# Packing the first row block of a float32 decoder trunk and fixing the order of its opening work

## The chip, the cores and the metric

The kernel runs on one core of one Trainium2 chip. The metric is the device time of one launch in microseconds, lower is better. It is measured from outside the program, so it is a little longer than the span in the profile, which runs from the first to the last instruction.

## The reference, cut to what matters

The program is one inference step of a one-layer convolutional decoder on 320 tokens (256 of a prompt, 8 groups of 8 new ones), all in float32:

```python
h = _rmsnorm(x, norm_mix_g)                      # x: 320 x 2048
proj = jnp.einsum('btd,dn->btn', h, w_in)        # w_in: 2048 x 14336
b_a, c_a, v_a, glu_a, glu_b, gate_a, gate_b = jnp.split(proj, IN_SPLITS, axis=-1)
conv_a, new_a = _causal_depthwise(c_a * v_a, buf_a, conv_a_w)
y_a = jnp.einsum('btc,cd->btd', b_a * conv_a, w_out_a)
u = glu_a * jax.nn.sigmoid(glu_b)
conv_b, new_b = _causal_depthwise(u, buf_b, conv_b_w)
...
x = x + jnp.einsum('btd,de->bte', merged, w_o)
h2 = _rmsnorm(x, norm_ffn_g)
ff = jax.nn.silu(jnp.einsum('btd,df->btf', h2, w_gate)) * jnp.einsum('btd,df->btf', h2, w_up)   # width 5632
x = x + jnp.einsum('btf,fd->btd', ff, w_down)    # then the final _rmsnorm
```

## The kernel before

**Products.** Every projection is computed in split precision: a weight w and an activation x are each cut into a "hi" part, rounded to TensorE's float32r, and a "lo" part, the float32 rest. Three products, hi·hi, hi·lo and lo·hi, stand for one (lines 221 to 223: `whi` with `rh`, `whi` with `rl`, `wlo` with `rh`). Each takes a stationary 128 x 128 weight tile and 320 moving columns, the tokens. Weights come from memory once, in *pieces* of 512 KB: four row slices k of 128 rows, 256 columns wide (tile `raw`, five buffers). ScalarE casts a piece to `whi` (line 181), VectorE subtracts to get `wlo` (line 185); there are three buffers of each. A *unit* is one output block of 256 columns; it has two accumulators in PSUM (one for each half j) and, for 2048 input rows, four pieces.

**The opening.** The weights cannot wait for the norm of x, so the first units multiply the x that is scaled by the norm's gain alone; the factor `rb`, one over the root mean square, is applied to the results. x is laid out as 16 chunks of 128 features by 320 tokens. For a chunk c, `x_chunk` makes `rh` on ScalarE (line 319) and `rl` on VectorE (line 320), and `x_square` squares it on ScalarE (line 326) and adds it up in `lnacc` on VectorE (lines 298 and 300). After the sixteenth square `x_factor` computes `rb`; `x_norm` then makes the normalized chunks that all later units use.

The first three units (two blocks of `glu_b`, one of `glu_a`) run as a group, so that a chunk of x feeds three units at once: `run_group` goes through row block 0 (chunks 0 to 3) slice by slice over the three units, and through row blocks 1 to 3 unit by unit. The callback `at_start(r, m, k)` is called ahead of row block r, unit m, slice k, and issues the x work and the splits of row block 0. From the fourth unit on, units run one after the other; each splits two pieces ahead and lets background tasks run (the 31-tap convolution of `glu_a * sigmoid(glu_b)` on VectorE, line 394, after ScalarE has copied its input into a window buffer `win`, line 386).

**What sets the order.** A list scheduler orders each engine's instructions by its own estimate of times; `tc.issue_after(x)` is a constraint on that order. At run time every engine works through its list in order and waits on semaphores. SyncE's queue issues nearly all transfers in program order, and each transfer uses one of eight semaphores in turn, so the ninth waits for the first. Ahead of the first product TensorE runs eleven products of an all-zero tile (`spin`, line 86), which VectorE clears first (line 83).

**The first transfers.** `lead` (the norm's gain and x chunk 0) on SyncE, the first slices of pieces 0 and 1 on ScalarE's queue, and then on SyncE, in turn, slices of pieces 0 to 2 and chunks of x, each its own transfer of 128 to 256 KB.

Of the kernel before, what the change touches and what calls it, by code (L numbers as in the profile page):

```python
# [8 lines left out]
F32 = mybir.dt.float32  # L9
# [3 lines left out]
ALU = mybir.AluOpType  # L13
# [19 lines left out]
SLOTS = 100  # L33
# [5 lines left out]
def trunk_kernel(ctx: ExitStack, tc: tile.TileContext, a):  # L39
# [33 lines left out]
    def xcol(c):  # L73
        return a["x"][:, NC + c * T : NC + (c + 1) * T]

    def load_x(cs):
        for c in cs:
            xc[c] = slot("xc")
            sp.dma_start(out=xc[c], in_=xcol(c))  # L79


    idle = slot("idle", F32R)
    ve.memset(idle.bitcast(F32), 0.0)
    o = pst("spin")
    for _ in range(11):
        first = te.matmul(o[:, :T], idle[:, 0:P], idle, start=True, stop=True, skip_group_check=True).ins
# [71 lines left out]
    def split_to(i):  # L158
        while nsplit[0] <= min(i, len(pieces) - 1):
# [7 lines left out]
            if nsplit[0] == 3:  # L167
                split(q, 0, 2)
                split(q, 2, 4)
            elif nsplit[0] > 3:  # L170
                split(q, 0, n)
# [6 lines left out]
    def hi_part(q, k0, k1, eng=None):  # L178
        ks = slice(k0, k1)
        f = ve.tensor_copy if eng is ve else ac.copy  # L180
        return f(out=q["hi"][:, ks, :], in_=q["raw"][:, ks, :]).ins  # L181
# [29 lines left out]
    def begin(u):  # L211
# [4 lines left out]
        def prod(q, k, j):  # L216
# [4 lines left out]
            te.matmul(o, wh, hi[kk], start=(kk == 0), stop=False)  # L221
            te.matmul(o, wh, lo[kk], start=False, stop=False)  # L222
            return te.matmul(o, wl, hi[kk], start=False, stop=(kk == nk - 1)).ins  # L223
# [5 lines left out]
    def run_group(us, at):  # L229

        on = [begin(u) for u in us]
        steps = [(0, m, k) for k in range(KP) for m in range(3)]
        steps += [(r, m, k) for r in range(1, NC // KP) for m in range(3) for k in range(KP)]
        for r, m, k in steps:
# [3 lines left out]
            if r:  # L238
                load_to(pi + DMA_AHEAD)
            at(r, m, k)  # L240
            if r and k == 0 or (r, m, k) == (0, 1, KP - 1):
                with tc.issue_after(x_last["ac"]), tc.issue_after(x_last["ve"]):
                    split_to(pi + 1 if r else 3)
# [52 lines left out]
    def csum(dst, src, c):  # L296
        if c == 0:
            ve.tensor_copy(out=dst, in_=src)
        else:
            ve.tensor_tensor(out=dst, in0=dst, in1=src, op=ALU.add)  # L300
# [748 lines left out]
```

## Time and profile before

| | us |
|---|---|
| median of 3 runs | 2079.13 |
| lowest and highest run | 2079.02, 2079.3 |
| the profiled execution | 2079.16 |
| its span | 2077.4 |
| TensorE busy | 2066.7 (99%) |
| VectorE busy | 1269.2 (61%) |
| ScalarE busy | 806.3 (39%) |

The profiled execution's time is 1.76 us more than its span; what is said of the span holds for the time when that difference stays. TensorE is called PE in the profile (PEld are its weight loads), VectorE DVE, ScalarE ACT, GpSimd POOL, SyncE SP; a q behind a name is that engine's queue of transfers. A row of the timeline gives the start and the duration in us, the engine, the line, the operation, out<-in, the shapes, how many instructions in a row were merged, and in brackets how long the engine was idle before and what ended that. Products overlap in the pipeline, so the pace is read from start to start, not from durations. A row of the tile view gives count, then least, median and longest duration in ns, then the first and the last start. A row of the window view gives the stretch, its length, the busy time of the five engines, TensorE's granted clock, the transfer engines' share, and GB/s.

### The profile page before, as it was taken

How to read it: one execution, taken by the hardware profiler on the slowest of the kernel's cores; microseconds unless marked ns; L12 is line 12 of the kernel's file. 1: busy time of each engine (PE TensorE's matmuls, PEld its weight loads, DVE VectorE, ACT ScalarE, POOL GpSimd, SP SyncE). 2: the span in 40 equal slices, each digit the busy share in tenths (PEclk: the TensorE clock that was granted, in tenths of full speed). 3: DMA queues.
4: the chain of work that ended last, by engine and by line, in shares of the span. 5: the costliest groups of instructions: out<-in, count | busy, mean ns of one | idle time of the engine just before them, and what ended most of it. 6: DMA issues, size and time to landing. Idle time of an engine off the chain costs nothing.

```text
span 2077.4 us, 33904 instructions
## 1 busy us (share of the span) xinstructions
PE 2066.7 (99%) x14097; PEld 2064.1 (99%) x14097; DVE 1269.2 (61%) x1854; ACT 806.3 (39%) x1170; POOL 4.4 (0%) x26
## 2 busy tenths in 40 slices
PE   9999999999999999999999999999999999999998
PEld 9999999999999999999999999999999999999998
DVE  7898889988986754345555645545334544544445
ACT  6544344444434344333344333333223333333432
POOL 0000000000000000000000000000000000000000
PEclk9999999999999999999999999999999999999999
DMA  8555544444444444444555444444454444444553
GB/s 268 155 173 155 183 143 153 153 152 145 155 152 150 145 151 153 149 147 151 158 172 169 151 152 148 148 151 147 143 157 152 152 149 147 151 152 143 153 149 107
DMA packets 98050, 321.17 MB, mean 155 GB/s; under 512 B 12936, under 2 KB 21192, under 8 KB 97864
## 3 DMA queue, kind: packets, MB, share of 16 engines
q1 hardware_dynamic: 97320, 318.35, 49.3%
q8 instruction: 110, 1.80, 0.4%
q10 hardware_dynamic: 576, 0.66, 0.1%
q14 instruction: 44, 0.36, 0.0%
HBM read 315.42 MB, written 4.98 MB: 154 GB/s over the span
## 4 chain that ended last, share of the span: by engine, by line
PE 99%; DMA 1%; DVE 0%; ACT 0%; SPq 0%; issue 0%; DVEq 0%
PE acc L223 33%; PE acc L221 33%; PE acc L222 32%; DMA raw<-in_w_in 1%; PE acc L695 0%; PE acc L697 0%; PE acc L696 0%; PE acc L700 0%; PE acc L701 0%; DVE yo L790 0%; DVE rl L320 0%; PE rbp L820 0%; DVE wlo L185 0%; SPq L146 0%; SPq L79 0%
## 5 line engine op out<-in xcount | busy, mean ns | idle before, releaser
L185 DVE TENSOR_TENSOR wlo<-raw,whi 128x1024 fp32r<-128x1024 f32 (+1 forms) x602 | 717.3, 1192 | 706.6 <-ACT whi L181 702.6
L181 ACT CAST whi<-raw 128x1024 fp32r<-128x1024 f32 (+2 forms) x601 | 615.6, 1025 | 1179.0 <-PE acc L222 925.4
L222 PE MATMUL acc<-hl,whi 128*128 128x320 f32 x1600 | 494.2, 309 | 0.0
L221 PE MATMUL acc<-hh,whi 128*128 128x320 f32 x1600 | 493.8, 309 | 0.0
L223 PE MATMUL acc<-hh,wlo 128*128 128x320 f32 x1600 | 493.4, 309 | 0.0
L223 PE MATMUL acc<-gh,wlo 128*128 128x320 f32 x1408 | 435.1, 309 | 0.0
L221 PE MATMUL acc<-gh,whi 128*128 128x320 f32 x1408 | 435.1, 309 | 0.0
L222 PE MATMUL acc<-gl,whi 128*128 128x320 f32 x1408 | 435.1, 309 | 0.0
L222 PEld LDWEIGHTS acc<-hl,whi 128*128 128x128 f32 x1600 | 300.3, 188 | 0.0
L221 PEld LDWEIGHTS acc<-hh,whi 128*128 128x128 f32 x1600 | 300.2, 188 | 0.0
L223 PEld LDWEIGHTS acc<-hh,wlo 128*128 128x128 f32 x1600 | 300.1, 188 | 0.0
L222 PEld LDWEIGHTS acc<-gl,whi 128*128 128x128 f32 x1408 | 264.3, 188 | 0.0
L221 PEld LDWEIGHTS acc<-gh,whi 128*128 128x128 f32 x1408 | 264.3, 188 | 0.0
L223 PEld LDWEIGHTS acc<-gh,wlo 128*128 128x128 f32 x1408 | 264.3, 188 | 0.0
L394 DVE SCALAR_TENSOR_TENSOR cb<-win,prm,cb 128x320 f32<-128x320 f32 x480 | 257.4, 548 | 7.4
L221 PE MATMUL acc<-fh,whi 128*128 128x320 f32 x660 | 203.9, 309 | 0.0
L222 PE MATMUL acc<-fl,whi 128*128 128x320 f32 x660 | 203.9, 309 | 0.0
L223 PE MATMUL acc<-fh,wlo 128*128 128x320 f32 x660 | 203.9, 309 | 0.0
L221 PEld LDWEIGHTS acc<-fh,whi 128*128 128x128 f32 x660 | 123.9, 188 | 0.0
L222 PEld LDWEIGHTS acc<-fl,whi 128*128 128x128 f32 x660 | 123.9, 188 | 0.0
L223 PEld LDWEIGHTS acc<-fh,wlo 128*128 128x128 f32 x660 | 123.9, 188 | 0.0
L221 PE MATMUL acc<-zh,whi 128*128 128x320 f32 x256 | 79.1, 309 | 0.0
(175 smaller groups left out, 2032.3 us busy)
## 6 DMA issues: line engine op xcount, KB each, us to landing
raw<-in_w_in SPq DMA_DIRECT2D x221, 512.0 KB, 3.7
raw<-in_w_gate SPq DMA_DIRECT2D x88, 512.0 KB, 3.6
raw<-in_w_up SPq DMA_DIRECT2D x88, 512.0 KB, 3.6
raw<-in_w_down SPq DMA_DIRECT2D x80, 512.0 KB, 3.6
raw<-in_w_out_a SPq DMA_DIRECT2D x32, 512.0 KB, 3.6
raw<-in_w_out_b SPq DMA_DIRECT2D x32, 512.0 KB, 3.5
raw<-in_w_o SPq DMA_DIRECT2D x32, 512.0 KB, 3.6
raw<-in_w_down SPq DMA_DIRECT2D x16, 256.0 KB, 2.7
```

Source lines behind the costliest of these rows:

```text
L181: return f(out=q["hi"][:, ks, :], in_=q["raw"][:, ks, :]).ins
L185: return ve.tensor_tensor(out=q["lo"][:, ks, :], in0=q["raw"][:, ks, :], in1=q["hi"][:, ks, :].bitcast(F32), op=ALU.subtract).ins
L221: te.matmul(o, wh, hi[kk], start=(kk == 0), stop=False)
L222: te.matmul(o, wh, lo[kk], start=False, stop=False)
L223: return te.matmul(o, wl, hi[kk], start=False, stop=(kk == nk - 1)).ins
L394: ve.scalar_tensor_tensor(out=o, in0=win[0][:, :, j + 2 : j + 10], scalar=w_cb(j, c), in1=o, op0=ALU.mult, op1=ALU.add)
```

## The change

The host packs what the first row block needs into three new inputs, in the order of need: `op0` is the gain, chunk 0 and slice 0 of the first unit; `op1` is slice 0 of the other two units; `op2` holds, for each of slices 1 to 3, the chunk of x and the slices of all three units side by side. They are loaded with seven transfers, `op0` and `op1` in halves of 64 partitions on SyncE and ScalarE. They land in two tiles that take over buffers used late in the program (`opening` that of the convolution's window, `xone`, for chunks 4 to 9, one that the last stage uses). Products of slice 0 are ordered hi·hi for all three units, then hi·lo, then lo·hi. ScalarE and VectorE take the opening's x chunks, squares and splits in an order fixed by two tables. The spinning products read a constant.

```diff
-    lead = const.tile([P, NC + T], F32, name="lead")
-    gmix, xc[0] = lead[:, 0:NC], lead[:, NC : NC + T]
-    sp.dma_start(out=lead, in_=a["x"][:, 0 : NC + T])
+    W = T + 3 * NB
+    lead = const.tile([P, NC + T + NB], F32, name="lead")
+    opening = io.tile([P, 2 * D], F32, tag="pair", name="opening")
+    xone = io.tile([P, D], F32, tag="one", name="xone")
+    gmix, xc[0], opened[0][0] = lead[:, 0:NC], lead[:, NC : NC + T], lead[:, NC + T :]
...
+    for eng, h in ((sp, slice(0, P // 2)), (aq, slice(P // 2, P))):
+        eng.dma_start(out=lead[h], in_=a["op0"][h])
+        warmed = eng.dma_start(out=opening[h, 0 : 2 * NB], in_=a["op1"][h]).ins
+    for k in range(1, KP):
+        o = opening[:, 2 * NB + (k - 1) * W : 2 * NB + k * W]
+        sp.dma_start(out=o, in_=a["op2"][k - 1])
+        xc[k] = o[:, 0:T]
+        for m in range(3):
+            opened[m][k] = o[:, T + m * NB : T + (m + 1) * NB]
...
-    idle = slot("idle", F32R)
-    ve.memset(idle.bitcast(F32), 0.0)
-    o = pst("spin")
-    for _ in range(11):
-        first = te.matmul(o[:, :T], idle[:, 0:P], idle, start=True, stop=True, skip_group_check=True).ins
+    idle = nc.const_aps.tensor(0.0, (P, 1), F32)
+    o = pst("spin")
+    for _ in range(14):
+        first = te.matmul(
+            o[:, :64], idle.broadcast_to((P, P)), idle.broadcast_to((P, 64)), start=True, stop=True, skip_group_check=True
+        ).ins
...
-        steps = [(0, m, k) for k in range(KP) for m in range(3)]
-        steps += [(r, m, k) for r in range(1, NC // KP) for m in range(3) for k in range(KP)]
-        for r, m, k in steps:
+        for k in range(KP):
+            u0 = [pieces[u["pieces"][0]] for u in us]
+            for f in (0, 1, 2) if k == 0 else (None,):
+                for m in range(3):
+                    if not f:
+                        at(0, m, k)
+                    with tc.issue_after(last_mm[0]):
+                        for j in range(2):
+                            last = on[m][1](u0[m], k, j, f)
+                    last_mm[0] = last
+        for r, m, k in [(r, m, k) for r in range(1, NC // KP) for m in range(3) for k in range(KP)]:
...
-        x_last["ac"] = ac.activation(out=r_hi[c], in_=xc[c], func=AF.Copy, scale=g_mix(c)).ins
+        if c == 0:
+            x_last["ve"] = ve.tensor_scalar(out=r_hi[c], in0=xc[c], scalar1=g_mix(c), scalar2=None, op0=ALU.mult).ins
+        else:
+            x_last["ac"] = ac.activation(out=r_hi[c], in_=xc[c], func=AF.Copy, scale=g_mix(c)).ins
...
+    def open_split(m, k):
+        q = pieces[m]
+        h = ac.copy(out=q["hi"][:, k, :], in_=opened[m][k])
+        l = ve.tensor_tensor(out=q["lo"][:, k, :], in0=opened[m][k], in1=q["hi"][:, k, :].bitcast(F32), op=ALU.subtract)
+        x_last["ac"], x_last["ve"] = h.ins, l.ins
+
+    x_at = [(1, 0, 0), (1, 0, 1), (1, 0, 3), (1, 1, 0), (1, 1, 2), (1, 2, 0), (1, 2, 2), (2, 0, 0), (2, 0, 2), (2, 1, 0)]
+    sq_at = [(0, 0, 2), (0, 0, 3), (1, 0, 2), (1, 1, 1), (1, 1, 3), (1, 2, 1), (1, 2, 3), (2, 0, 1), (2, 0, 3)]
...
+        if (r, m, k) in sq_at:
+            in_turn(x_square, sq_at.index((r, m, k)))
+        if (r, m, k) == (0, 1, KP - 1):
+            in_turn(x_chunk, 4)
+            split_to(3)
+            for h in (0, 2):
+                x_last["ac"] = in_turn(hi_part, pieces[3], h, h + 2)
+                x_last["ve"] = in_turn(lo_part, pieces[3], h, h + 2)
+            in_turn(x_chunk, 5)
+        if (r, m, k) in x_at:
+            in_turn(x_chunk, 6 + x_at.index((r, m, k)))
...
-    load_part(2, 0, 1, sp)
-    load_x((1,))
-    for i in range(3):
-        load_part(i, 1, 2, sp)
...
+    load_to(3)
+    load_x(4, 4)
+    load_to(5)
+    load_x(8, 2)
...
-            for c in range((base + n) * 14 // of, (base + n + 1) * 14 // of):
+            lo, hi = ((base + i) * 14 // of for i in (n, n + 1))
+            for c in range(max(lo, 2), max(hi, 2)) if base + n else range(2):
                 x_norm(2 + c)
```

In the order of instructions this shows at three places.

TensorE, the first products (the spin, then slice 0; `acc_156` to `acc_161` before and `acc_145` to `acc_150` now are the six accumulators, `whi` and `wlo` the parts of the three units' weights). Before:

```order
L86 MATMUL spin_80<-idle_78 128x320 x11
L221 MATMUL acc_156<-rh_162,whi_150 128x320
L221 MATMUL acc_157<-rh_162,whi_150 128x320
L222 MATMUL acc_156<-rl_163,whi_150 128x320
L222 MATMUL acc_157<-rl_163,whi_150 128x320
L223 MATMUL acc_156<-rh_162,wlo_151 128x320
L223 MATMUL acc_157<-rh_162,wlo_151 128x320
L221 MATMUL acc_158<-rh_162,whi_152 128x320
```

and now:

```order
L104 MATMUL spin_86<-const-float32-0.0 128x64 x14
L238 MATMUL acc_145<-rh_151,whi_139 128x320
L238 MATMUL acc_146<-rh_151,whi_139 128x320
L238 MATMUL acc_147<-rh_151,whi_141 128x320
L238 MATMUL acc_148<-rh_151,whi_141 128x320
L238 MATMUL acc_149<-rh_151,whi_143 128x320
L238 MATMUL acc_150<-rh_151,whi_143 128x320
L240 MATMUL acc_145<-rl_152,whi_139 128x320
```

The six hi·hi products of slice 0 stand ahead of the first that needs a lo part.

SyncE's transfers, from the first one. Before:

```order
L71 DMA lead<-in_x 128x336
L79 DMA xc_122<-in_x 128x320
L146 DMA raw_120<-in_w_in 128x256
L146 DMA raw_115<-in_w_in 128x256
L146 DMA raw_117<-in_w_in 128x256
L146 DMA raw_120<-in_w_in 128x256
L79 DMA xc_127<-in_x 128x320
L146 DMA raw_115<-in_w_in 128x512
L79 DMA xc_130<-in_x 128x320
L146 DMA raw_117<-in_w_in 128x512
L146 DMA raw_120<-in_w_in 128x512
L146 DMA raw_134<-in_w_in 128x1024
```

and now (`raw_125`, `raw_128` and `raw_130` are pieces 3 to 5, `xone` chunks 4 to 7):

```order
L78 DMA lead<-in_op 64x592
L79 DMA opening<-in_op 64x512
L82 DMA opening<-in_op 128x1088 x3
L166 DMA raw_125<-in_w_in 128x1024
L98 DMA xone<-in_x 128x1280
L166 DMA raw_128<-in_w_in 128x1024
L166 DMA raw_130<-in_w_in 128x1024
```

Eleven transfers ahead of piece 3 have become five, with two more on ScalarE's queue as before.

ScalarE at the start of row block 1. Before (`xc_136` to `xc_142` are chunks 4 to 7, `raw_134` and `raw_144` pieces 3 and 4):

```order
L319 ACTIVATE rh_258<-xc_136,lead 128x320
L181 CAST whi_152<-raw_117 128x256
L319 ACTIVATE rh_270<-xc_138,lead 128x320
L181 CAST whi_154<-raw_120 128x256
L326 ACTIVATE sq_274<-xc_127 128x320
L319 ACTIVATE rh_291<-xc_140,lead 128x320
L326 ACTIVATE sq_295<-xc_130 128x320
L326 ACTIVATE sq_322<-xc_136 128x320
L319 ACTIVATE rh_335<-xc_142,lead 128x320
L181 CAST whi_277<-raw_134 128x512 x2
L181 CAST whi_325<-raw_144 128x1024
```

and now:

```order
L348 ACTIVATE rh_257<-xone,lead 128x320
L197 CAST whi_261<-raw_125 128x512 x2
L348 ACTIVATE rh_267<-xone,lead 128x320
L197 CAST whi_293<-raw_128 128x1024
L348 ACTIVATE rh_297<-xone,lead 128x320
L348 ACTIVATE rh_307<-xone,lead 128x320
L355 ACTIVATE sq_317<-opening 128x320
```

Piece 3's split stands ahead of all but the first of the four chunks, and piece 4's split ahead of the third and the fourth. VectorE's list has the same order of chunks and pieces.

More of the change, by code (lines that the diff above doesn't have):

```diff
@@ L32 @@
 SPL_BUFS = 3
-SLOTS = 100
+SLOTS = 99
 DMA_AHEAD = 4
@@ L220, in prod @@
             o = acc[j][:, :T]
-            te.matmul(o, wh, hi[kk], start=(kk == 0), stop=False)
-            te.matmul(o, wh, lo[kk], start=False, stop=False)
-            return te.matmul(o, wl, hi[kk], start=False, stop=(kk == nk - 1)).ins
+            if which in (None, 0):
+                last = te.matmul(o, wh, hi[kk], start=(kk == 0), stop=False)
+            if which in (None, 1):
+                last = te.matmul(o, wh, lo[kk], start=False, stop=False)
+            if which in (None, 2):
+                last = te.matmul(o, wl, hi[kk], start=False, stop=(kk == nk - 1))
+            return last.ins
         return acc, prod
@@ L237, in run_group @@
             acc, prod = on[m]
-            if r:
-                load_to(pi + DMA_AHEAD)
+            load_to(pi + DMA_AHEAD)
+            if k == 0:
+                with tc.issue_after(x_last["ac"]), tc.issue_after(x_last["ve"]):
+                    split_to(pi + 1)
             at(r, m, k)
-            if r and k == 0 or (r, m, k) == (0, 1, KP - 1):
-                with tc.issue_after(x_last["ac"]), tc.issue_after(x_last["ve"]):
-                    split_to(pi + 1 if r else 3)
             with tc.issue_after(last_mm[0]):
@@ new lines, in trunk_kernel @@
+    sq_at += [(2, 1, 1), (2, 1, 2), (2, 1, 3), (2, 2, 0), (2, 2, 1), (2, 2, 2), (2, 2, 3)]
+    def at_start(r, m, k):
+        if (r, m) == (0, 0):
+            if k == 0:
+                with tc.issue_after(warmed_act.ins):
+                    x_chunk(0)
+                    x_last["ac"] = warmed_act.ins
+            else:
+                in_turn(x_chunk, k)
+            for i in range(3):
+                in_turn(open_split, i, k)
+        if (r, m, k) in sq_at:
[9 more added lines that the diff above has]
+            in_turn(x_chunk, 6 + x_at.index((r, m, k)))
@@ L998, in _lay_in @@
     x = np.concatenate([f["x_prompt"].reshape(TP, D), f["x_sample"].reshape(TS, D)])
-    o["x"] = np.concatenate([_rows(np, f["norm_mix_g"]).reshape(P, NC), _rows(np, x).reshape(P, NC * T)], axis=1)
+    xr = _rows(np, x)
+    o["x"] = xr.reshape(P, NC * T)
+    w = o["w_in"]
+    first = [w[n // NB, :, 0:KP] for n in (4 * D, 3 * D, 4 * D + NB)]
+    o["op0"] = np.concatenate([_rows(np, f["norm_mix_g"]).reshape(P, NC), xr[:, 0], first[0][:, 0]], axis=1)
+    o["op1"] = np.concatenate([first[1][:, 0], first[2][:, 0]], axis=1)
+    o["op2"] = np.stack([np.concatenate([xr[:, k]] + [v[:, k] for v in first], axis=1) for k in range(1, KP)])
     names = ("final_norm_g", "norm_ffn_g", "conv_b_bias", "ln_b_g", "ln_b_b", "conv_a_w", "conv_b_w")
```

84 lines of the change are left out of this document (31 added, 53 removed).

## The prediction

> **What bounds the kernel now.** I read the page's head first, then the chain that ended last, then TensorE's waits, and at last the first 20 us in the timeline.
>
> ```profile
> span 2077.4 us, 33904 instructions
> PE 99%; DMA 1%; DVE 0%; ACT 0%; SPq 0%; issue 0%; DVEq 0%
> PE rbp L820 <- DVE rst L790: 1.6, 1, 1.6
> PE spin L86 <- DVE idle L83: 1.2, 1, 1.2
> PE acc L221 <- ACT whi L181: 0.9, 1, 0.9
> PE acc L223 <- DVE wlo L185: 0.2, 1, 0.2
> ```
>
> The second row is the chain: TensorE is 99% of it. The next four are all that the wait view puts down to TensorE: 1.6 us in the tail, and 1.2, 0.9 and 0.2 us at the front. So a change to the front can win back only what the front loses. Some losses are spread too thin for that view; the timeline of TensorE shows them:
>
> ```profile
> 1.25 3.30 PE L86 MATMUL spin<-idle 128*128 128x320 f32 x11 [1.25 <-DVE idle L83]
> 4.63 0.78 PE L221 MATMUL acc<-rh,whi 128*128 128x320 f32 x2
> 5.24 0.53 PE L222 MATMUL acc<-rl,whi 128*128 128x320 f32 x2
> 5.61 0.50 PE L223 MATMUL acc<-rh,wlo 128*128 128x320 f32 x2
> ...
> 7.70 0.46 PE L221 MATMUL acc<-rh,whi 128*128 128x320 f32 x2
> ...
> 17.75 0.41 PE L221 MATMUL acc<-rh,whi 128*128 128x320 f32 x1 [0.90 <-ACT whi L181]
> ...
> 19.23 0.31 PE L221 MATMUL acc<-rh,whi 128*128 128x320 f32 x1
> ...
> 999.84 0.31 PE L223 MATMUL acc<-zh,wlo 128*128 128x320 f32 x1
> ...
> 1002.92 0.31 PE L223 MATMUL acc<-zh,wlo 128*128 128x320 f32 x1
> ```
>
> The last two rows are 21 products apart: 3.08 / 21 = 0.1467 us each, the steady pace. Row block 0 is 72 products, 10.56 us at that pace. It starts at 4.63 and row block 1 starts at 17.75, so 2.56 us are lost in it. The six products from 17.75 to 19.23 take 1.48 us where 0.88 is the pace: another 0.60. **The front loses 3.16 us after its first product**, and whatever the first product could start earlier comes on top. Behind 19.23 the wait view has only the tail, and the pace holds to there: from 17.75 to the tail's transposes lie 13,820 such products (13,884 in all, less 72, and eight for the sums),
>
> ```profile
> 2045.46 0.65 PE acc L708 x6
> ```
>
> which is 2027.71 us less the 0.60, or 0.1467 for each.
>
> Why block 0 is late stands in ScalarE's and VectorE's rows: they wait for weights.
>
> ```profile
> 4.01 0.56 ACT L319 ACTIVATE rh<-lead 128x320 fp32r<-128x320 f32 x1 [0.86 <-DMA lead<-in_x]
> 4.19 0.29 DVE L181 CAST whi<-raw 128x256 fp32r<-128x256 f32 x1 [2.99 <-DMA raw<-in_w_in]
> 4.60 0.55 DVE L320 SCALAR_TENSOR_TENSOR rl<-lead,rh 128x320 fp32r<-128x320 f32 x1
> 4.98 0.73 ACT L181 CAST whi<-raw 128x256 fp32r<-128x256 f32 x2 [0.41 <-DMA raw<-in_w_in]
> 8.87 0.41 ACT L181 CAST whi<-raw 128x256 fp32r<-128x256 f32 x1 [0.85 <-DMA raw<-in_w_in]
> 10.85 0.41 ACT L181 CAST whi<-raw 128x256 fp32r<-128x256 f32 x1 [1.57 <-DMA raw<-in_w_in]
> 17.09 2.07 ACT L181 CAST whi<-raw 128x512 fp32r<-128x512 f32 x3
> 2.00:4.00 2.00, 2.00 (x9) 2.00 (x9) 0.00 (x0) 1.14 (x2) 0.00 (x0) 1.00 0.89 290
> 4.00:6.00 2.00, 1.92 (x10) 1.41 (x9) 1.69 (x5) 1.58 (x4) 0.00 (x0) 1.00 0.98 301
> 8.00:10.00 2.00, 2.00 (x16) 2.00 (x15) 0.98 (x3) 0.43 (x2) 0.00 (x0) 1.00 0.99 249
> 20.00:25.00 5.00, 5.00 (x36) 5.00 (x36) 5.00 (x9) 5.00 (x10) 0.00 (x0) 1.00 1.04 384
> ```
>
> The last number of the four window rows is GB/s: 249 to 301 while the small first pieces (1 KB a partition and row) come in, 384 with whole pieces, the DMA engines full in both. At 17.09 piece 3 is split on ScalarE behind the x chunks.
>
> **The first products.** Before them come lead, 168 KB, and one 128 KB weight slice; the packed op0 is 296 KB (592 x 4 B x 128), the same.
>
> ```profile
> lead<-in_x SPq DMA_DIRECT2D x1, 168.0 KB, 3.3
> raw<-in_w_in ACTq DMA_DIRECT2D x2, 128.0 KB, 3.6
> ```
>
> I take its landing as before, 4.05 us (bounds 3.7, since rows are longer, and 4.4). Then ScalarE's cast (0.41) and VectorE's x0 run side by side where they ran on swapped engines: first product 4.5 against 4.63. [...] op1 (256 KB) lands at 4.4 to 5.0: the same bytes were moved by 4.0, and the last cast that waited for them starts at 4.98. Two more casts (0.73 for two) follow; the six hi products end by about 5.6, the lo ones need x0's lo (0.55) and three subtractions of 0.35. All 18 products end at 7.5 to 7.7, and 7.70 is when the second slice starts before. **Gain of this part 0.1 us**, from -0.2 to 0.3: the new order swaps one wait for another.
>
> **Row block 0, slices 1 to 3.** Each comes as one 544 KB transfer (557 kB), behind nothing else. 580 kB have moved by 4.0 us (290 GB/s for 2 us) and some 20 before. From there I take 350 GB/s: the rows above bound it by 249 and 384, and 4.3 KB a row is nearer to the whole pieces. To that comes the time to signal: lead and the first weights, 303 kB, have moved by about 3.1 at 290 GB/s, and their readers go at 4.01 and 4.19; other bytes ran between them, so 0.4 to 1.0, and I take 0.7. The slices land at 6.2, 7.8 and 9.4 us. A slice's x and first cast take 0.56 + 0.41, so 1.0 us, and the products ask for them at 7.6, 10.2 and 12.9. No wait is left, even at 270 GB/s (6.6, 8.7, 10.8). **Gain 2.1**, all of what slices 1 to 3 lose before: 17.75 - 7.70 less 54 products at the pace (7.92). Row block 1 then asks at 15.5.
>
> **Row block 1.** Piece 3 (524 kB) lands at 10.9 and x4 to x7, now one transfer of 655 kB, at 12.7. The half split of piece 3 is ready 0.56 + 0.69 later, 14.0, in time, so the 0.60 goes. But ScalarE and VectorE run in order, and x6 now stands behind piece 4:
>
> ```profile
> L185 DVE TENSOR_TENSOR wlo<-raw,whi 128x1024 fp32r<-128x1024 f32 (+1 forms) x602 | 717.3, 1192 | 706.6 <-ACT whi L181 702.6
> L181 ACT CAST whi<-raw 128x1024 fp32r<-128x1024 f32 (+2 forms) x601 | 615.6, 1025 | 1179.0 <-PE acc L222 925.4
> ```
>
> x4 (0.56), two halves (1.38), x5 (0.56), piece 4's cast (1.03), its subtraction (1.19) and x6's lo (0.55) are 5.3 us; instructions that follow each other overlap by some 0.1, twice here, so 5.1. x6's lo is ready 5.1 us after x4's landing, 17.8, and TensorE asks for it 14 products after 15.5, at 17.55. **A new wait of 0.25 us**; later landings add to it us for us: 0 at 384 GB/s, 1.0 at 320. I take 0.6 (x4 at 13.05, 336 GB/s). Behind it the pieces are two ahead, as before.
>
> **The spin.** Eleven 320-column float32r products become fourteen 64-column float32 ones. They read a constant, so the 1.2 us wait for VectorE's memset goes:
>
> ```profile
> 0.23 0.10 POOL L1038 MEMSET const-float32-0.0<- 128x1 f32 x1 [0.23 <-issue]
> 0.87 0.33 DVE L83 MEMSET idle<- 128x320 f32 x1 [0.87 <-PEq L1038]
> ```
>
> TensorE, released with VectorE, can start near 0.85. What one costs is not in the trace; the rows nearest are the cold spin and the tail's float32 sums, three instructions that show as six records:
>
> ```profile
> L86 PEld LDWEIGHTS spin<-idle x11: 289/334/338, 1.2 to 3.8; 128*128 128x128 f32 x11
> L86 PE MATMUL spin<-idle x11: 472/472/637, 1.2 to 4.1; 128*128 128x320 f32 x11
> 2053.51 0.74 PEld L767 LDWEIGHTS pv<-ones,lnacc 128*128 128x128 f32 x6
> L767 PEld LDWEIGHTS pv<-ones,lnacc x6: 133/189/192, 2053.5 to 2054.1; 128*128 128x128 f32 x4, 128*64 128x64 f32 x2
> ```
>
> So 28 records. Lower bound, by columns: the old spin went at (4.1 - 1.2) / 10 = 0.29 for 320, so 0.06 for 64, 28 of them 1.6 us, ending at 2.5. Upper bound, by weight loads: 0.74 / 6 = 0.123 a record at the full clock, and 334 / 189 as much in the cold: 0.22. With the clock rising 4.0 us after the start (before: 1.25 to the change of pace between 5.24 and 5.61) 18 records are cold and ten warm: 0.85 + 4.0 + 1.2 = 6.1 us. The row of the weight loads is nearest in kind, but whether a load is slower in the cold is what it does not show; without that, 0.85 + 28 x 0.123 = 4.3. I take 4.3, just in time; 6.1 is a rival. [...]
>
> **The rest** I cost at nothing. Waiting for the window buffer (it now holds x1 to x3 until the third is normalized) delays the first convolution copies,
>
> ```profile
> 55.92 1.62 ACT L386 COPY win<-up 128x224 f32<-128x224 f32 x5
> 60.28 1.04 ACT L181 CAST whi<-raw 128x1024 fp32r<-128x1024 f32 x1
> ```
>
> but TensorE did not wait in that burst of 4.4 us between two casts, since two pieces (24 products each, 7.0 us) are split ahead, and the new burst is as long. If that cover were gone it would cost 1 to 2 us. The tail keeps its order on every engine.
>
> **Sum**, against the profiled execution, 2079.16 us (0.03 above the median of the runs, so no correction): -0.1 (first products) -2.1 (block 0) -0.6 (start of block 1) +0.6 (x6) = -2.2, **2077.0 us**, -0.11%. Its own range is 2076.1 to 2077.4.
>
> **Rivals.**
> *The spin holds TensorE to 6.1.* For it: float32 records come in pairs, and the cold load lasted 334 ns. Against: a load's length may be waiting. Then all 18 first products run at the pace, end at 8.75, row block 1 starts at 16.7 and x6 is in time: the 78th product falls at 17.5 instead of 19.23, 2077.5.
> *The spin ends too early.* If it ends at 2.5, TensorE idles for 2 us and its products may start at the cold pace, 0.30 each (two from 4.63 to 5.24), until 4.0 us after 4.5. The hi products wait for op1 anyway; eight products from 6.0 to 8.5 cost 0.15 more each: 2078.2. [...]
> *The transfers stay slow.* At 285 GB/s x4 lands at 14.6 and the wait for x6 is 2.1: 2078.5. For it: 249 to 301 between 4 and 10 us. Against: those were rows of 1 KB, and whole pieces came at 384.
> *Slower: piece 4 in front of x6.* The same in-order wait takes back all of 2.8 us once x4 lands later than 15.3, which takes less than 267 GB/s from 4 us on. At 250 it lands at 15.9, the wait is 3.5: 2079.9. For it: one stretch of 2 us at 249. Against: no 13 us in a row were so slow.
> *All goes well.* op0 lands at 3.7, first product at 4.15, no wait for x6: gain 3.2 + 0.4, 2075.6.
>
> **How the numbers follow.** Forecast 0.48; long spin 0.20; short spin 0.06; slow transfers 0.12; slower 0.06; all well 0.08. The range, 2075.9 to 2078.4, holds the forecast, both spin cases and parts of the slow transfers and of the all-well case, about 0.82. 0.2% is 4.2 us, about what a measurement of this kernel can tell from no change; the front has 3.16 us to give back, and even with a first product at 4.15 the gain stays below 3.7. So faster by over 0.2% gets 0.04; slower by over 0.2% would need 6 us of new waits, 0.02; within, 0.94.
>
> **What would show it.** Right: TensorE's first product at 4.4 to 4.6, the second slice near 7.6, row block 1 at 15.4 to 15.7 with no wait for piece 3, one short wait of an L240 product for x6's lo near 17.6, the steady pace by 20 and a span of about 2075.2. Spin records ending after 5 prove the second case. Wrong: any TensorE wait over 0.3 us between 8 and 15, 544 KB transfers landing later than 7, 9 and 11 us, or a difference of the two traces behind 50 us.

## The result and the profile after

The changed kernel takes 2081.66 us (median of 22 runs, 2081.0 to 2083.15), the kernel before 2079.12 us on the same chip (22 runs, 2078.95 to 2080.1): a ratio of 1.0013, with a 95% interval of 1.0007 to 1.0019. The change was to win 2.2 us and loses 2.5. A few single executions that took over 100 us longer than the rest, of the kernel before and of the experiments h and l, are left out of all medians.

The profiled execution took 2082.48 us, 0.8 more than the median, with a span of 2080.3. So the span is 2.9 us longer than before, and the time outside of it 2.18 us where it was 1.76. The first rows to read are TensorE's waits:

```profile
PE rbp L849 <- DVE rst L819: 1.6, 1, 1.6
PE spin L104 <- PEq L1080: 0.8, 1, 0.8
PE rps L321 <- DVE s_lo L316: 0.7, 1, 0.7
PE acc L240 <- DVE rl L349: 0.4, 1, 0.4
```

The tail's 1.6 is unchanged, the wait for the memset has become 0.8, and both waits for weights are gone. Two new ones, 0.4 for x6's lo and 0.7 ahead of the sums, are 1.1 of the 2.9 us in this view. The rest is no wait. TensorE's timeline has it:

```profile
0.77 6.21 PE L104 MATMUL spin<-const-float32-0.0 128*128 128x64 f32 x28 [0.77 <-PEq L1080]
6.74 1.95 PE L238 MATMUL acc<-rh,whi 128*128 128x320 f32 x6
8.49 1.80 PE L240 MATMUL acc<-rl,whi 128*128 128x320 f32 x6
10.09 1.80 PE L242 MATMUL acc<-rh,wlo 128*128 128x320 f32 x6
11.69 0.58 PE L238 MATMUL acc<-rh,whi 128*128 128x320 f32 x2
...
19.73 0.31 PE L238 MATMUL acc<-rh,whi 128*128 128x320 f32 x1
...
20.61 0.46 PE L238 MATMUL acc<-rh,whi 128*128 128x320 f32 x2
...
22.35 0.42 PE L240 MATMUL acc<-rl,whi 128*128 128x320 f32 x1 [0.41 <-DVE rl L349]
```

The spin holds TensorE to 6.74, and the next 18 products go at 0.27 us each: the clock is not up. Slice 1 begins at 11.69 where it began at 7.70, 4.0 us late. Row block 0's other 54 products then take 8.04 us (10.05 before) and the six that follow 0.88 (1.48 before), so the 79th product starts at 20.61 instead of 19.23: 4.0 - 2.0 - 0.6 = 1.4 us late. The wait for x6's lo adds 0.57, read from start to start (22.35 - 20.61 less eight products). The tile view of the spin shows the 28 records' pace, 5.8 us over 27 steps, 0.215 us each, as long at the end as at the start:

```profile
L104 PEld LDWEIGHTS spin<-const-float32-0.0 x28: 288/333/338, 0.7 to 6.5; 128*128 128x128 f32 x28
L104 PE MATMUL spin<-const-float32-0.0 x28: 421/421/447, 0.8 to 6.6; 128*128 128x64 f32 x28
```

TensorE's lateness covers a second thing. ScalarE's timeline has the first readers of op0, op1 and slice 1; the window view has the transfers' rate as its last number:

```profile
4.32 0.41 ACT L892 CAST whi<-lead 128x256 fp32r<-128x256 f32 x1 [0.86 <-DMA lead<-in_op]
5.58 0.71 ACT L892 CAST whi<-opening 128x256 fp32r<-128x256 f32 x2 [0.86 <-DMA opening<-in_op]
8.97 0.56 ACT L348 ACTIVATE rh<-opening,lead 128x320 fp32r<-128x320 f32 x1 [2.68 <-DMA opening<-in_op]
```

```profile
2.00:5.00 3.00, 3.00 (x16) 3.00 (x16) 0.62 (x2) 1.86 (x3) 0.00 (x0) 1.00 0.88 228
```

Slice 1 is read at 8.97, not at 6.2. With a first product at 4.5, TensorE would have had to wait for it.

The wait ahead of the sums, in the timeline of the three engines, first of the change and then of the kernel before:

```profile
41.57 1.05 ACT L197 CAST whi<-raw 128x1024 fp32r<-128x1024 f32 x1 [2.47 <-PE acc L240]
42.52 0.46 ACT L315 CAST s_hi<-lnacc 128x320 fp32r<-128x320 f32 x1
42.65 1.23 DVE L201 TENSOR_TENSOR wlo<-raw,whi 128x1024 fp32r<-128x1024 f32 x1 [2.29 <-ACT whi L197]
43.79 0.49 DVE L316 TENSOR_TENSOR s_lo<-lnacc,s_hi 128x320 fp32r<-128x320 f32 x1
44.33 0.42 PE L321 MATMUL rps<-s_lo,ones_r 128*128 128x320 f32 x1 [0.75 <-DVE s_lo L316]
```

```profile
38.22 0.48 DVE L289 TENSOR_TENSOR s_lo<-lnacc,s_hi 128x320 fp32r<-128x320 f32 x1
41.38 0.31 PE L294 MATMUL rps<-s_lo,ones_r 128*128 128x320 f32 x1
```

The halves of the sum of squares now stand behind the split of piece 11, which must wait 2.47 us for TensorE to free a buffer. Before they stood behind piece 10's, and s_lo was done at 38.7, in time for its product at 41.38. From start to start the wait costs 1.0 us: the two sums take from 43.27 to 44.58 now and took from 41.22 to 41.52 before. (The view's 0.7 is only the idle time.)

### The profile page after: what moved, and what is told of

The parts are those of the page before. It is cut to its first block, busy times and chain, and to the rows that moved or that the text cites. A ratio compares the mean times of both kernels' runs of the same rounds, so it can differ in the third digit from the quotient of the medians.

```text
span 2080.3 us, 33923 instructions
## 1 busy us (share of the span) xinstructions
PE 2070.3 (100%) x14114; PEld 2069.2 (99%) x14114; DVE 1268.5 (61%) x1853; ACT 806.2 (39%) x1170; POOL 4.5 (0%) x26
## 2 busy tenths in 40 slices
DMA packets 96354, 321.17 MB, mean 154 GB/s; under 512 B 12776, under 2 KB 18984, under 8 KB 96168
## 4 chain that ended last, share of the span: by engine, by line
PE 99%; DVE 0%; ACT 0%; issue 0%; DVEq 0%
PE acc L240 33%; PE acc L238 33%; PE acc L242 33%; PE spin L104 0%; PE acc L724 0%; PE acc L726 0%; PE acc L725 0%; PE acc L729 0%; PE acc L730 0%; ACT whi L197 0%; DVE yo L819 0%; DVE wlo L201 0%; PE rbp L849 0%; PE acc L737 0%; DVEq L1087 0%
## 5 line engine op out<-in xcount | busy, mean ns | idle before, releaser
L197 ACT CAST whi<-raw 128x1024 fp32r<-128x1024 f32 (+1 forms) x590 | 611.8, 1037 | 1172.3 <-PE acc L240 931.1
L238 PE MATMUL acc<-ah,whi 128*128 128x320 f32 x256 | 79.1, 309 | 0.0
```

The lines of the kernel that those rows point to most:

```text
L197: return ac.copy(out=q["hi"][:, ks, :], in_=q["raw"][:, ks, :]).ins
L238: last = te.matmul(o, wh, hi[kk], start=(kk == 0), stop=False)
```

## The experiments

The theories. **S**: the spin's light products hold TensorE and leave the clock low. **L**: the late transfers are a second cause. **W**, formed after the first runs: the clock changes only at steps 3.413 us apart (from the clock records, below), whose phase differs from launch to launch, and it rises at a step if TensorE streamed enough in the *window* since the step before. **Q**: the transfers are late because the opening is cut over two queues. Each kernel is compared with the kernel before on its chip, 2079.0 to 2079.3. Most ratios have intervals of about ±0.1%, 2 us, so one comparison rarely parts two kernels. What follows rests on the traces and on medians of ten runs.

### The spin, four ways

`a_old_spin`, the changed kernel with the spin of before:

```diff
-    idle = nc.const_aps.tensor(0.0, (P, 1), F32)
+    idle = slot("idle", F32R)
+    ve.memset(idle.bitcast(F32), 0.0)
...
-    for _ in range(14):
-        first = te.matmul(o[:, :64], idle.broadcast_to((P, P)), idle.broadcast_to((P, 64)), ...
+    for _ in range(11):
+        first = te.matmul(o[:, :T], idle[:, 0:P], idle, ...
```

> The changed kernel with the spin of the kernel before (eleven 320-column float32r products of a tile that VectorE clears). Theory S, the spin is the cause: the first product goes back from 6.74 to about 4.6, the clock rises about 5.3 instead of 12, the 18 products of slice 0 end at 7.7 instead of 11.7, and the rest of the prediction's sum comes out: a span near 2075.5, 2077.2 us in all. Theory L, the landings are a second cause that the spin only covers: the three 544 KB slices land as in the changed kernel (last parts at about 9.0, 10.3 and 11.7), slice 1 is asked for at 7.7 and its first cast is done at 9.9, so TensorE waits some 2 us there, row block 1 starts near 17.9, as before, and the 0.7 us ahead of the sums stays: 2078.8 to 2079.4, no gain over the kernel before.

Measured: 2081.42 (2079.17 to 2083.11). Its trace is of an execution at 2079.71, and reads as L says in kind: first product at 4.67, the second unit's weights awaited for 0.48, slice 1 for 0.31 (L expected 2 us), row block 1 at 16.98 (L: 17.9), the 0.7 ahead of the sums still there. But the ten times lie in two groups, three of them to 2079.9 and seven from 2081.2, so the median misses both forecasts. S alone falls.

`b_new_spin`, the kernel before with the change's spin (the reverse of that diff):

> The kernel before with the spin of the change alone (28 records of 64-column float32 products of a constant). Theory S: 28 loads of 0.216 us hold TensorE to 6.7, the clock stays low to about 12 us, the first 18 products end near 11.7 instead of 7.7; the four later weight waits of row block 0 (2.6 us) are then covered, so row block 1 starts near 11.7 + 54 x 0.147 = 19.6 instead of 17.75: 1.9 us slower, less the 0.6 us behind it, 2080.2 to 2081.0. The rival, that the late clock comes from the order of the first products and not from the spin: first product near 6.7 but the clock up by 6.9 (four us of spin), 2079.2 to 2079.6.

Measured: 2079.70 (2079.21 to 2080.52); in its trace (2080.34) the spin ends as in the changed kernel, slice 1 begins at 11.64, row block 1 at 19.56, and the 79th product at 20.44, 1.2 us later than before. That is S in kind; but the median loses only 0.5, less than S forecast and no clear loss (ratio 1.0003, 0.9994 to 1.0013).

`c_spin_f32_320`, six float32 products of 320 columns, and `d_spin_f32r_64`, 28 float32r products of 64 columns of a cleared tile (as in a, with `range(28)` and `idle[:, 0:64]`). The diff is c's:

```diff
-    for _ in range(14):
-        first = te.matmul(o[:, :64], ..., idle.broadcast_to((P, 64)), ...
+    for _ in range(6):
+        first = te.matmul(o[:, :T], ..., idle.broadcast_to((P, T)), ...
```

> The changed kernel with six spinning products of 320 columns in place of fourteen of 64, still float32 and still of the constant: 12 records. If the clock rises by the columns that stream through the array (64 columns of each 0.216 us load are too few), it rises about 4 us after the spin's start, near 5, and the first products run at 0.147 soon after: 2077.5 to 2079.5, as with the old spin. If it is float32, or the constant operand, that does not count as work for the clock, it rises only near 10 to 12 us and the time stays at 2080 to 2081.5.

> The changed kernel with 28 float32r spinning products of 64 columns, read from a cleared tile: as many records as the change's spin has, of one pass each. If the weight loads set their pace, a record again takes about 0.216 us and the spin ends near 7.2. If few streamed columns are what leaves the clock low, it rises only near 12 again: 2081.5 to 2082.2. If the type is the cause, it rises near 5.2, the last records go at 0.12, the first product comes near 5.5: 2078 to 2079.5.

Measured: c 2080.08 (2079.67 to 2080.48), d 2082.19 (2081.81 to 2083.16; ratio 1.0015, 1.0006 to 1.0025). TensorE's timeline, of c and then of d:

```profile
0.77 5.97 PE L104 MATMUL spin<-const-float32-0.0 128*128 128x320 f32 x12 [0.77 <-PEq L1080]
6.34 1.28 PE L238 MATMUL acc<-rh,whi 128*128 128x320 f32 x6
7.46 1.04 PE L240 MATMUL acc<-rl,whi 128*128 128x320 f32 x6
```

```profile
1.25 6.18 PE L105 MATMUL spin<-idle 128*128 128x64 f32 x28 [1.25 <-DVE idle L102]
7.25 1.95 PE L237 MATMUL acc<-rh,whi 128*128 128x320 f32 x6
8.99 1.80 PE L239 MATMUL acc<-rl,whi 128*128 128x320 f32 x6
```

With 320 columns the first products soon go at 0.147; with 64 they go at 0.27 to 0.29 until the clock rises at 10.94, 3.7 us after the first. c's time alone would fit the rival (2080 to 2081.5), since its twelve records, which start 0.53 us apart in the cold, hold TensorE to 6.34; its clock, up at 5.83, decides. Both types and both operands were tried at 64 columns (the change and d, clock up at 11.95 and 10.94) and at 320 (c, a and e, up at 5.83, 5.33 and 5.64): here type and operand do not matter, the columns of a product do. A record of 64 columns takes 0.21 us in float32r too (5.8 us over 27 steps). So its columns do not set its pace: at the cold pace 64 of 320 are 0.06 us in float32r (0.29 for 320) and 0.11 in float32 (0.53), a quarter and a half of 0.21. That the weight load sets it is an estimate by exclusion; no run varies the load.

### When the clock rises

The trace also records when TensorE's clock changes (the window view's column prints 1.00 for cold stretches too, so its pace must be read from start to start). In us from the span's start:

```
clock up at
spin of 64 columns:  before's order (b) 11.58; the change 11.95; d 10.94; f 9.19; g 11.82; m 10.31
spin of 320 columns: before 5.12; a 5.33, again 5.40; c 5.83; e 5.64; i 4.70; j 5.89; l 5.30; n 5.72; o 3.82; p 3.94
h: up at 4.89, down at 8.31, up at 11.72
```

The two groups do not touch. The clock records have full speed for 2065.063 us in the change and for 2068.477 us in the kernel before, which are 605 and 606 times 3.4133, and h's times are 3.42 and 3.41 apart: in these traces the clock changes at steps of 3.413 us. Where the steps lie differs from launch to launch: less whole steps, the rises of the table lie from 0.07 us (m) to 2.48 us (j) behind the span's start. Behind the wide spins, which began at 0.77 or 1.25, the clock rose at 3.8 to 5.9. In o the window ahead of the rise began at 0.41 and the spin at 0.77, so it need not be full. In the change the window from 5.1 to 8.5 held light records and 1.8 us of products, and the clock did not rise behind it. In f it rose behind a window, from 5.8 to 9.2, with light records and 2.45 us of products. That the work in the window decides is W's reading of these traces; how much is enough no run shows.

`a_again` was to show an execution of a's upper group:

> The changed kernel with the spin of the kernel before once more, for a second trace: its ten times lay in two groups, 2079.2 to 2079.9 (the trace taken was one of these) and 2081.2 to 2083.1. [...]

It took 2080.13, between the groups: clock up at 5.40, slice 1 awaited for 0.78. What makes a's upper group no trace shows; h, below, shows one way.

### Dense spin, order, one input

`e_dense`: 18 float32r products of 320 columns of the constant, no memset.

```diff
-    idle = nc.const_aps.tensor(0.0, (P, 1), F32)
+    idle = nc.const_aps.tensor(0.0, (P, 1), F32).bitcast(F32R)
...
-    for _ in range(14):
-        first = te.matmul(o[:, :64], ..., idle.broadcast_to((P, 64)), ...
+    for _ in range(18):
+        first = te.matmul(o[:, :T], ..., idle.broadcast_to((P, T)), ...
```

> The changed kernel with 18 float32r spinning products of 320 columns of the constant: no wait for VectorE, no float32 pairs, and TensorE busy without a gap from 0.8 to about 5 or 6. [...] Slice 1's landing then sets the pace from about 8.9, as in the changed kernel with the old spin, row block 1 starts near 17; with the 0.4 for x6, the 0.7 ahead of the sums and 0.4 more outside of the span than before that is 2079.2 to 2080.0. Theory S alone (only the spin was wrong): no wait for slice 1, 2077.0 to 2078.0. If the constant read with stride zero does not count for the clock, 2081 or more.

Measured: 2080.35, and the ten times lie within 0.65 us (2080.02 to 2080.67), as W would have it of a spin with no gap. It is 0.35 above the upper end of the forecast because op1 came later still, with TensorE waiting:

```profile
5.68 0.46 PE L238 MATMUL acc<-rh,whi 128*128 128x320 f32 x2
7.52 0.87 PE L238 MATMUL acc<-rh,whi 128*128 128x320 f32 x4 [1.38 <-ACT whi L892]
```

`f_order`: the two places put back.

```diff
-            if k == 0:
-                with tc.issue_after(x_last["ac"]), tc.issue_after(x_last["ve"]):
-                    split_to(pi + 1)
             at(r, m, k)
+            if k == 0:
+                with tc.issue_after(x_last["ac"]), tc.issue_after(x_last["ve"]):
+                    split_to(pi + 1)
...
             in_turn(x_square, sq_at.index((r, m, k)))
+            if sq_at.index((r, m, k)) == NC - 1:
+                in_turn(halves, lnacc)
...
     def x_factor():
         p = pst("rps")
-        halves(lnacc)
```

> The changed kernel with two places of the order put back: x chunk work of a row block's first slice ahead of the next piece's split (so x6 ahead of piece 4), and the halves of the sum of squares right behind the sixteenth square, ahead of the splits of pieces 10 and 11. Its spin stays. If the two waits after 20 us are causes of their own, the 0.4 ahead of an L240 product and the 0.7 ahead of the second sum go, and nothing takes their place: 1.1 us less than the changed kernel's 2081.66, 2080.5, with the same spread. If TensorE only meets the next late thing (piece 4, or the factor), 2081.2 to 2081.8.

Measured: 2080.06. Both waits are gone from TensorE's list, and in that list none came in their place:

```profile
PE rbp L848 <- DVE rst L818: 1.6, 1, 1.6
PE spin L104 <- PEq L1081: 0.8, 1, 0.8
```

The gain on the changed kernel is 1.6, 0.5 more than the forecast from the idle time of the two waits. Read from start to start the waits cost 0.57 and 1.0; but the medians of ten runs with this spin also scatter by about 0.5 (g and m have 2082.2 and 2081.7), and in f's trace the clock rose early, at 9.19.

`g_one_input`: the packed columns in x's array (`a["x"][h, 0:OP1]` for `a["op0"][h]`, and so on). Here and in h the residual at the end takes other columns of that array for four chunks of x, which changes no instruction.

> The changed kernel with the packed columns kept in the array of x, one input in place of four; transfers, their sizes and their order stay. The changed kernel's time is 2.2 us more than its span, that of the kernel before 1.76. If the three added inputs cost that, the difference goes back to 1.76 and the time to 2081.2; if it comes from the kernel's code or queues, it stays at 2.2 and the time at 2081.66. The span should not move beyond the spread, since a row of 2 to 4 KB is read in one piece either way.

Measured: 2082.22, and 2.11 to 2.23 us outside of the span in all ten runs. The number of inputs is not what costs the 0.4 us. The page counts 96,354 DMA packets, as the change's does, whose op2 is 384 packets of 4,352 bytes: a row is read in one piece either way.

`h_all`: e, f and g together.

> All three together: 18 dense spinning products, the two places of the order put back, and one input. If the causes add: the dense spin takes 1.9 off the changed kernel's 2081.66, the order 1.1, the input 0.4, so 2078.2, 1.0 us below the kernel before (ratio 0.9995). If the landing of slice 1 is worth more than thought, or a wait takes the place of those two, 2079 to 2079.6, level with the kernel before.

Measured: 2080.29, in two groups, five runs at 2078.7 to 2079.7 and five at 2080.9 to 2081.8. The causes did not add, and the trace, of an execution of the upper group (2081.43), shows why:

```profile
0.77 4.71 PE L107 MATMUL spin<-const-float32-0.0 128*128 128x320 f32 x18 [0.77 <-PEq L1084]
5.32 0.45 PE L241 MATMUL acc<-rh,whi 128*128 128x320 f32 x2
8.19 1.35 PE L241 MATMUL acc<-rh,whi 128*128 128x320 f32 x4 [2.41 <-ACT whi L894]
9.34 1.80 PE L243 MATMUL acc<-rl,whi 128*128 128x320 f32 x6
```

op1 came at 7.7, and TensorE stood still for 2.41 of the 3.42 us from the clock's rise at 4.89 to its fall at 8.31; the products that followed went at 0.27 to 11.7. A late transfer costs twice here. Not every gap does: in e the 3.41 us from the rise at 5.64 had the wait of 1.38 us and some 2.0 us of products in them, and the clock stayed up.

### Where the transfers were late

Over the nine traces with the change's transfers, op1's first reader started at 5.4 to 7.7 (median 6.1) and slice 1's at 7.8 to 9.0 (8.3). `i_one_queue` is e with whole transfers on SyncE's queue:

```diff
-    for eng, h in ((sp, slice(0, P // 2)), (aq, slice(P // 2, P))):
-        eng.dma_start(out=lead[h], in_=a["op0"][h])
-        warmed = eng.dma_start(out=opening[h, 0 : 2 * NB], in_=a["op1"][h]).ins
+    sp.dma_start(out=lead, in_=a["op0"])
+    warmed = sp.dma_start(out=opening[:, 0 : 2 * NB], in_=a["op1"]).ins
```

> The changed kernel with the 18 dense spinning products, and op0 and op1 as whole transfers on SyncE's queue, none on ScalarE's. Theory Q (op1's half on ScalarE's queue shares the transfer engines with the first 544 KB slice, which SyncE issues 0.6 us behind it, and lands with it): with one queue op1 comes ahead of the slice, its first reader starts at 5.0 to 5.6 in every run instead of 5.6 to 7.7, TensorE's wait of 1.4 us for the second unit's weights goes, slice 1 (first cast 8.9) becomes what TensorE waits for, and the time falls from 2080.35 to about 2079.7. If the halves land late for another reason (too many bytes in all), the reader stays at 6 to 7.5 and the time at 2080.2 to 2080.6. Without a transfer on ScalarE's queue it also shows whether the 0.36 us outside of the span come from there: 1.8 instead of 2.15.

Measured: 2078.68 (2078.14 to 2079.47), 1.7 below e (1.5 when each is set against the kernel before on its chip) and 1.0 below the forecast. Both readers are early, op1's at 4.33 and slice 1's at 5.68:

```profile
4.33 0.71 ACT L891 CAST whi<-opening 128x256 fp32r<-128x256 f32 x2 [0.25 <-DMA opening<-in_op]
...
5.68 0.56 ACT L347 ACTIVATE rh<-opening,lead 128x320 fp32r<-128x320 f32 x1 [0.63 <-DMA opening<-in_op]
```

Outside of the span it still takes 2.11 to 2.22 us, without a transfer on ScalarE's queue. Two runs part the queue from the cut; in their diffs the lines that i takes out go as well. `l_halves` keeps the halves of 64 partitions, on one queue:

```diff
+    both = (slice(0, P // 2), slice(P // 2, P))
+    for h in both:
+        sp.dma_start(out=lead[h], in_=a["op0"][h])
+    for h in both:
+        warmed = sp.dma_start(out=opening[h, 0 : 2 * NB], in_=a["op1"][h]).ins
```

> The changed kernel with the 18 dense spinning products, and op0 and op1 in halves of 64 partitions as in the change, but all four halves on SyncE's queue. If it is the second queue that makes the opening late (its packets take turns with SyncE's in the same 16 transfer engines), the landings are those of the whole transfers on one queue, a little later for two more issues (0.4 us each): op1's first reader at 4.8 to 5.4, slice 1's near 6.5, 2078.7 to 2079.3. If it is the halves, the readers stay at 6 to 7.5 and near 8, 2080.2 to 2080.6.

`p_columns` keeps both queues and cuts by columns, 128 partitions each:

```diff
+    for eng, c0, c1, d in ((sp, 0, NC + T, 0), (aq, NC + T, NC + T + NB, NB)):
+        eng.dma_start(out=lead[:, c0:c1], in_=a["op0"][:, c0:c1])
+        warmed = eng.dma_start(out=opening[:, d : d + NB], in_=a["op1"][:, d : d + NB]).ins
```

> The changed kernel with the 18 dense spinning products, and op0 and op1 still on two queues at once, but cut by columns: each transfer fills half of the columns of all 128 partitions. Halves of 64 partitions cost something even on one queue (issue 0.61 us against 0.39, 197 to 223 GB/s between 2 and 5 us against 245 to 432). [...] If it is the second queue that takes turns with SyncE's, the readers stay at 5.5 to 7 and near 8, 2080.0 to 2080.6.

Measured: l 2079.07, p 2079.23. The window view of l, p and i, in this order, and then an issue on SyncE's queue and the first readers of op1 and slice 1 from the timeline of l and of p:

```profile
2.00:5.00 3.00, 3.00 (x13) 3.00 (x13) 0.63 (x2) 0.62 (x3) 0.00 (x0) 1.00 0.83 207
```

```profile
2.00:5.00 3.00, 3.00 (x16) 3.00 (x16) 1.19 (x4) 2.15 (x5) 0.00 (x0) 1.00 1.00 339
```

```profile
2.00:5.00 3.00, 3.00 (x14) 3.00 (x14) 1.28 (x4) 1.28 (x5) 0.00 (x0) 1.00 0.99 365
```

```profile
0.73 1.22 SPq L79 DMA_DIRECT2D lead<-in_op  x2
5.49 0.71 ACT L894 CAST whi<-opening 128x256 fp32r<-128x256 f32 x2 [0.77 <-DMA opening<-in_op]
7.16 0.56 ACT L350 ACTIVATE rh<-opening,lead 128x320 fp32r<-128x320 f32 x1 [0.95 <-DMA opening<-in_op]
```

```profile
0.73 0.39 SPq L78 DMA_DIRECT2D lead<-in_op  x1
4.39 0.71 ACT L892 CAST whi<-opening 128x256 fp32r<-128x256 f32 x2
7.11 0.56 ACT L348 ACTIVATE rh<-opening,lead 128x320 fp32r<-128x320 f32 x1 [2.00 <-DMA opening<-in_op]
```

Neither theory holds alone. op1 is late by the cut: its first reader starts at 5.49 in l and at 4.39 in p, where i has 4.33, so Q falls in its first form. Slice 1 is late by both: 7.16 in l and 7.11 in p, where i has 5.68 and e, with both, 8.41. By time, set against the kernel before on its chip, e is 1.1 us slower, l 0.1 faster, p 0.1 slower and i 0.4 faster: either edit alone brings back most of what both do. l's time is the one that was forecast if the second queue is the cause; p's is 0.8 below the one that was forecast if it is. In the change's trace packets of the two queues do go side by side: from 2.5 to 4.0 us 96 start on ScalarE's and 89 on SyncE's. These are single traces, and the five kernels with one queue and whole transfers read slice 1 at 5.7 to 7.0 (and op1 at 4.3 to 4.5), so the second queue's share of p's 7.11 may be small.

In the trace the halves cost two things. A half takes 0.61 us to issue where a whole takes 0.39, so l issues slice 1 at 3.28 and i at 1.64. And from 2 to 5 us 207 GB/s are moved on one queue and 228 on two (the change), against 339 and 365 with 128 partitions; in l a part of that is the later issue. Why 64 partitions are slower no trace shows, neither with the halves one after the other (l) nor with both under way at once (the change).

`m_queue_only` and `n_old_spin_queue` are i's edit on the changed kernel with its own spin, and with the spin of before:

> The changed kernel with op0 and op1 as whole transfers on SyncE's queue, and nothing else: the spin of the change stays. If the spin hides the landings, as its trace says (TensorE did not wait between 6.7 and 20 us), the earlier landings gain nothing before x6, 6.74 and the late clock stay, the wait for x6's lo (0.4) may go: 2081.2 to 2081.9. If the transfers are the whole cause, 2078.7.

> The changed kernel with the spin of the kernel before and with one queue for op0 and op1: both suspected causes in the opening undone. If these two are the whole of it, the first product comes near 4.5, slices 1 to 3 are in time, and what is left of the prediction's sum against the kernel before is -2.8 of the front, +0.4 for x6, +0.7 ahead of the sums, +0.36 outside of the span: 2077.8, and all ten times within 1 us. If the old spin, which ends at 4.4, leaves a gap that costs the clock in some launches, a second group near 2079.5.

Measured: m 2081.74, as forecast: earlier transfers alone bring nothing while the spin holds TensorE. n 2078.44 (2077.99 to 2079.42), 0.6 above its forecast; seven times lie at 2078.0 to 2078.7 and three at 2079.1 to 2079.4, and whether these are the second group of the forecast's rival no trace shows. TensorE's timeline of n:

```profile
4.36 1.77 PE L236 MATMUL acc<-rh,whi 128*128 128x320 f32 x6
...
7.72 0.46 PE L236 MATMUL acc<-rh,whi 128*128 128x320 f32 x2
...
18.26 0.42 PE L238 MATMUL acc<-rl,whi 128*128 128x320 f32 x1 [0.41 <-DVE rl L347]
```

Slice 1 begins at 7.72, row block 1 at 15.64 and the 79th product at 16.52, 2.7 us earlier than before; with the wait for x6's lo 2.0 remain at the 97th. That is the front that was predicted (2.2 with x6's wait in it). The sums' 1.0 and the 0.4 outside take it down to 0.7 in this execution (2078.48 against 2079.16).

### The best version

`j_best` has i, f's two places, and chunk 1's rh on VectorE (`if c < 2` for `if c == 0` in `x_chunk`). `o_best13` is j with 13 spinning products.

> The dense spin, one queue for the opening, the two places of the order put back, and chunk 1's rh on VectorE as chunk 0's is (so that it stands beside slice 1's first cast and not ahead of it). If the causes add: 2079.7 less 1.1 to 1.6 for the two waits and less 0.4 for the cast, 2077.8 to 2078.3, a ratio of 0.9995, and no TensorE wait left in the front but that for slice 1, near 0.5. If the clock then falls or rises late in some launches, two groups 1.5 us apart.

> As the best kernel so far (2077.54), with 13 spinning products in place of 18. Theory W: what fills the window may as well be the products themselves; the spin then ends at 4.5 whatever the phase, the hi products are ready (first cast done at 4.2, all by 5.2), and work that was done from 5.3 to 5.9 on is done from 4.5 on, in part at the slow pace: 0.4 to 0.8 us less, 2076.8 to 2077.2. If a gap behind the shorter spin keeps the clock down in some launches, or slice 1 (first reader at 5.7 to 7.0) becomes what TensorE waits for, 2077.4 to 2078.5.

Measured: j 2077.54 (ratio 0.9992, 0.9983 to 1.0001), o 2077.24 (ratio 0.9991, 0.9982 to 1.0000), both in one group, o's from 2076.61 to 2078.16. j is 0.3 better than its forecast, o just above its own. TensorE's timeline of o:

```profile
0.77 3.50 PE L103 MATMUL spin<-const-float32-0.0 128*128 128x320 f32 x13 [0.77 <-PEq L1080]
4.21 0.52 PE L237 MATMUL acc<-rh,whi 128*128 128x320 f32 x2
4.89 0.87 PE L237 MATMUL acc<-rh,whi 128*128 128x320 f32 x4 [0.16 <-ACT whi L890]
```

Row block 1 begins at 15.47, no wait for x6 or the sums is left, and the span is 2074.7, 2.7 below before; the time outside takes 0.4 of it back. So the change wins about 1.9 us in the median once its spin, its cut and its order are mended, and the interval just touches no gain. How much of that the kernel before would win from the new spin alone was not run; n, with the old spin, wins 0.8, no clear gain.

## Why the prediction was wrong

- **The spin's end is the step that failed**: taken at 4.3, bounded by 6.1, measured 6.74. The 4.3 used 0.123 us a record, the pace of the tail at the full clock, for a spin that starts cold; it went at 0.215. The 0.22 of the upper bound was right; that bound fell because it let ten of the 28 records run warm, 4.0 us after the start. No record ran warm. The clock was taken to follow time spent spinning; c, d and the table of clock times show it to follow the columns that stream (320: up at 5.83 in c; 64: at 10.94 in d). (The lower bound took a float32r pace, 0.29 for 320 columns, for float32 products; c has 0.53.)
- **First products, -0.1**: +4.0 (11.69 for 7.70), 2.1 from the late start and 1.9 from 18 products at 0.27. The rival of the long spin had the late start, but gave the products the warm pace; the rival of the cold pace had it after a spin that was too short. Neither was the case, and no rival joined the two, so the range ended at 2078.4.
- **Row block 0, -2.1, and the start of block 1, -0.6**: -2.0 and -0.6. Right in size, in part for another reason: slices at 6.2, 7.8 and 9.4 were wanted, slice 1 was read at 8.97, and TensorE was too late to notice. The step that gave the halves no cost of their own was wrong: op0, taken to land at 4.05, is read at 4.11 to 4.59 with halves on two queues and at 3.67 to 3.83 with whole transfers on one, and by the medians op1 is read 1.7 us and slice 1 1.6 us later than with whole transfers. With whole transfers (n) the steps come out: 7.72 for 7.6, 15.64 for 15.5.
- **x6's lo behind piece 4, +0.6**: 0.57. The place in the order is right, and f shows it; the size is luck. The sum let the wait follow x4's landing, us for us. ScalarE's rows, below, of the change and then of n, show what else stands between. x4 was read at 14.77, not 13.05, and piece 3's split then waited 2.69 us for a product of TensorE, which still read one of the three split buffers. In n x4 came 1.9 us earlier; the split waited for TensorE all the same, and x6's wait is again 0.57. It hangs on when TensorE frees a buffer, which the sum left out.
- **The rest at nothing**: wrong by 1.0 at the sums, whose halves stand behind piece 11's split; f shows the cause. Outside of the span 0.4 more were not foreseen. They come neither from the number of inputs (g) nor from ScalarE's queue (i) nor from the spin (b has 1.74 to 1.83 there); where they come from stays open.

```profile
14.77 0.56 ACT L348 ACTIVATE rh<-xone,lead 128x320 fp32r<-128x320 f32 x1 [0.84 <-DMA xone<-in_x]
18.02 1.14 ACT L197 CAST whi<-raw 128x512 fp32r<-128x512 f32 x2 [2.69 <-PE acc L240]
```

```profile
12.86 0.56 ACT L346 ACTIVATE rh<-xone,lead 128x320 fp32r<-128x320 f32 x1 [0.62 <-DMA xone<-in_x]
13.93 1.14 ACT L195 CAST whi<-raw 128x512 fp32r<-128x512 f32 x2 [0.51 <-PE acc L238]
```

The terms measured: 4.0 - 2.0 - 0.6 + 0.57 + 1.0 = 3.0, where the span has 2.9, plus 0.4 outside: 3.3 in the profiled execution, 2.5 in the median. Under "What would show it", spin records after 5 were to prove the long-spin rival; they came, with its price wrong. Of the marks for a failure one came: slice 1, to land by 7, was read at 8.97 as soon as it was there. The other, a TensorE wait between 8 and 15, did not come, since a slow clock is no wait.

## What to carry to other kernels

A warm-up is worth what it streams: give it wide products with no gap (here the clock rose at 3.8 to 5.9 us behind 320 columns, at 9.2 to 12.0 behind 64), let it end when the real ones are ready, and read the clock from the pace of the products behind it (0.27 us or 0.147), not from a list of waits. Cut a transfer by columns, or not at all, before cutting its partitions (op1 was read at 4.39 or 4.33, against 5.49). Here whole transfers on one queue were earliest (slice 1 at 5.68, against 7.11 to 8.41). When splits or squares move, look for what the scheduler has put behind a split that must wait for a buffer (2.47 us ahead of the sums).

## What was not expected of the hardware

- In these traces TensorE's clock changed at steps of 3.413 us (the change, before, h) with a phase of its own in each launch (0.07 to 2.48 us): up at 3.8 to 5.9 us behind a spin of 320 columns, at 9.2 to 12.0 behind one of 64, and down again after 2.41 us without work (h). That the phase is also what spreads the runs (3.9 us in a, 2.2 in the change, 0.65 in e, 1.2 in the kernel before) is likely but not shown, with one or two traces of each kernel.
- Transfers of 64 partitions: 0.61 us to issue against 0.39 (l, i), and 207 to 228 GB/s against 339 to 365 in the same 3 us (l and the change, p and i).
- A record of a float32 or float32r product of 64 columns cost 0.21 us in the cold (the change, d); one of 320 columns cost 0.53 in float32 (c) and 0.27 in float32r (e).
